# Second block's attention: both compressions in the two halves of the array, and the values' products of two units at once

## The chip, the cores and the metric

The kernel runs on one NeuronCore of a Trainium2 chip. The metric is the device time of one execution in microseconds (us), the median of repeated runs.

## The reference, cut to what matters

Two networks run one after the other on a sequence of 512 tokens of width 1024; the change lies in the second one, `second_block`, which has two layers. Each layer's mixer has four branches of width 512: native sparse attention (`o_a`), a convolution, a pooling mixer, and sliding-window attention (`o_d`).

```python
def nsa_compress(k, pos, w1, w2):              # for the keys and again for the values
    blk = jnp.swapaxes(k[:, idx], 2, 3) + pos  # 31 blocks of 32 positions, 2 groups, 64 channels
    flat = blk.reshape(bsz, n_cmp, g, CMP_LEN * dk)
    return jax.nn.gelu(flat @ w1, approximate=True) @ w2      # 2048 -> 256 -> 64
...
o_cmp, p_cmp = nsa_compressed_attention(qa, k_cmp, v_cmp)
o_slc = nsa_selected_attention(qa_rot, rope(k_slc), v_slc, sel)
o_win = banded_attention(qa_rot, rope(k_win), v_win, NSA_WINDOW, None)
o_a = ga[0] * o_cmp + ga[1] * o_slc + ga[2] * o_win
o_d = banded_attention(qd, rope(k_d), v_d, SWA_WINDOW, sinks)
```

There are 8 query heads of width 64 over 2 groups of keys and values, and all of it is float32.

## The kernel before

Nearly all of the time goes into products with weights. A weight tile of 128x1024 is loaded into one of three `raw` buffers, rounded by ScalarE (line 88, into one of three `whi` buffers), and the rest is formed by VectorE (line 89, into one of three `wlo` buffers). `mm3` (lines 112 to 114) then makes three products for each pair of tiles, hi by hi, hi by lo and lo by hi. A projection (`proj`) is 24 such products of 512 columns for one bank of results; there are four banks (`mm`).

`mix2` is one layer's mixer. It has a first stretch, written out as a list of calls at its end: `compress_inputs` for keys and values, `keys`, `swa_query`, `conv_taps` (a projection pair whose 30 taps VectorE works off in portions, `some(n)`), `pool_part` (a projection, sums on VectorE, then a product at line 1252), `compress`, and `values_and_gates` (the values of all four token tiles and the gates, 96 products of 408 columns in four chunks of weights, lines 1361 to 1372). `compress(kv, ab)` is called for the keys and for the values. It is a generator: up to its first `yield` it loads 16 tiles of `w1` into the `L` and `pT` buffers (four of each) and makes 16 products of a 128x64 stationary tile with 256 columns (line 1405) in rows 0 to 63 of one bank, then the GELU; up to the second it turns the hidden values over (line 1419), up to the third it multiplies with `w2` (lines 1428 and 1433).

Behind it come 48 units of attention: 16 of the sliding window and 32 of the sparse attention. `attend` makes a unit's scores (line 1453) and the softmax; `tail` turns the probabilities over (line 1475) into two `pT` buffers; `times_values` multiplies them with the values (line 1484), group 0 into rows 0 to 63 of the bank `po` and group 1 into rows 64 to 127, in turn. The loop over `n` issues unit n's scores, unit n-1's turning, then a portion of other work (`filling`: one projection or pieces of the gates and branches), then unit n-1's values. `attend_coarse(j)` (lines 1487 to 1516) makes the attention over the compressed keys for four units at once. The build reorders independent instructions on each engine, so the order that counts is that of the built program.

Of the kernel before, what the change touches and what calls it, by code (L numbers as in the profile page):

```python
# [16 lines left out]
P = 128  # L17
# [13 lines left out]
class Net:  # L31
# [1151 lines left out]
    def mix2(self, l, after):  # L1183
# [174 lines left out]
        def values_and_gates():  # L1358

            banks = [self.mm_bank() for _ in n4]  # L1360
            for c in range(4):
                whi, wlo = self.weights(a["w_in_vg_2"][l, :, c * 816:(c + 1) * 816])
                for k, t in [(k, t) for t in n4 for k in range(2)] if c == 3 else [(k, t) for k in range(2) for t in n4]:
                    hi, lo = self.hk(2 * c + k)
                    ws = slice(k * 408, (k + 1) * 408)
                    self.mm3(banks[t][:, :408], (hi[:, sl[t]], lo[:, sl[t]]), (whi[:, ws], wlo[:, ws]),
                             2 * c + k == 0, 2 * c + k == KD - 1)
            for t in n4:
                A.copy(vt[:, t, :], banks[t][:, :384])
                A.activation(ga[t], banks[t][:, 384:408], AF.Tanh, scale=0.5)  # L1370
            V.tensor_scalar(gt_, gt_, 0.5, 0.5, ALU.mult, ALU.add)
            V.tensor_scalar(ga[0][:, :8], ga[0][:, :8], valid, None, ALU.mult)


        kc = mp.tile([P, 64], F32, name=f"kc{l}")
# [17 lines left out]
                                    pos[:, kv, 8 * e:8 * e + 8, None].to_broadcast([P, 8, 32 - e]), ALU.add)  # L1393
            return ab

        def compress(kv, ab):

            ph = self.aux()
            for c in range(8):
                w1 = ltile() if c % 2 else ptile()  # L1400
                nc.sync.dma_start(w1, a["nsa_cmp_w1_2"][l, kv][:, c * 512:(c + 1) * 512])
                for i in range(2):
                    lp = 2 * c + i
                    e = lp // 8
                    T_.matmul(ph[:64, :256], ab[e][:, lp % 8].rearrange("p g n -> p (g n)"), w1[:, i * 256:(i + 1) * 256],  # L1405
                              start=(lp == 0), stop=(lp == 15))
            x = ph[:64, :256]
            t, w2 = gtile(), gtile()
            t = t[:64, :256]
            A.activation(t, x, AF.Square)  # L1410
            V.tensor_scalar(t, t, 0.044715, 1.0, ALU.mult, ALU.add)
            V.tensor_tensor(t, t, x, ALU.mult)
            A.activation(t, t, AF.Tanh, scale=math.sqrt(2.0 / math.pi))
            stt(t, t, 1.0, x, ALU.add, ALU.mult)
            nc.sync.dma_start(w2, a["nsa_cmp_w2_2"][l])
            yield
            pt = self.aux()
            for hf in range(2):
                T_.transpose(pt[:, hf * 64:(hf + 1) * 64], t[:, hf * P:(hf + 1) * P], self.ident[:64, :64])
            both = tmp(2 * P)  # L1420
            A.copy(both.rearrange("p (f r n) -> p f r n", f=2, r=2),
                   pt[:, :P].rearrange("p (f n) -> p f n", f=2)[:, :, None, :].to_broadcast([P, 2, 2, 64]))
            hid = [both[:, sl[hf]] for hf in range(2)]
            yield
            pt = self.aux()
            if kv == 0:
                for hf in range(2):
                    T_.matmul(pt[:, :64], w2[:, sl[hf]], hid[hf][:, :64], start=(hf == 0), stop=(hf == 1))
                for g in range(2):
                    A.mul(kc[halves[g], 32 * g:32 * g + 32], pt[halves[g], 32 * g:32 * g + 32], 0.5)  # L1430
            else:
                for hf in range(2):
                    T_.matmul(pt[:, :64], hid[hf], w2[:, (2 + hf) * P:(2 + hf) * P + 64],
                              start=(hf == 0), stop=(hf == 1))
                for b in range(4):
                    A.mul(vc[32 * b:32 * b + 32, b // 2, 64 * (b % 2):64 * (b % 2) + 64], pt[32 * b:32 * b + 32, :64], 0.5)
            yield

        def ltile():
            return mp.tile([P, 512], F32, tag="L", name=self.nm("L"), bufs=4)  # L1440
# [2 lines left out]
            return mp.tile([P, 512], F32, tag="pT", name=self.nm("pT"), bufs=4)  # L1443

        def attend(qs, ks, k0, w, mask, sinks, gate, vals, po, i, coarse, last):


            mn = mp.tile([P, 4], F32, tag="mn", name=self.nm("mn"), bufs=4)
            cols, Ls = self.packed(), []
            pts = [cols(w) for _ in range(2)]  # L1450
            for g, pt in enumerate(pts):
                for b, k in enumerate(ks):
                    T_.matmul(pt, qs[g][:, sl[i]], k[g][:, k0:k0 + w], start=b == 0, stop=b == 1)  # L1453
            for g, pt in enumerate(pts):
                L, m, s = ltile(), mn[:, 2 * g:2 * g + 1], mn[:, 2 * g + 1:2 * g + 2]
                init = sinks[g] if sinks else 3e38
                V.tensor_tensor_reduce(L[:, :w], pt, mask, scale=1.0, scalar=init, op0=ALU.add, op1=ALU.min, accum_out=m)
                e = w
                if sinks:
                    V.tensor_copy(L[:, w:w + 1], init)  # L1460
                    e += 1
                A.activation(L[:, :e], L[:, :e], AF.Exp, bias=m, scale=-1.0, accum_out=s)
                V.reciprocal(s, s)
                if gate is None:
                    V.tensor_scalar(L[:, :w], L[:, :w], s, None, ALU.mult)
                else:
                    V.tensor_scalar(L[:, :w], L[:, :w], s, gate[g], ALU.mult, ALU.mult)
                Ls.append(L)

            def tail():  # L1470
                pT = []
                for g in range(2):
                    pt = self.aux()
                    for c in range(0, w, P):
                        T_.transpose(pt[:, c:c + P], Ls[g][:, c:c + P], self.ident)  # L1475
                    pT.append(ptile())
                    (V.tensor_copy if g and w > 2 * P else A.copy)(pT[g][:, :w], pt[:, :w])

                def times_values():
                    todo = list(coarse) if coarse else []  # L1480
                    todo += [[(vals(g, b), pT[g][:, b * P:(b + 1) * P]) for g in range(2)] for b in range(w // P)]
                    for b, pair in enumerate(todo):
                        for g, (v, p) in enumerate(pair):
                            T_.matmul(po[halves[g], sl[i]], v, p, start=b == 0 and coarse is not None,  # L1484
                                      stop=last and b == len(todo) - 1)
                return times_values
            return tail
# [89 lines left out]
                taps.pop(0)()  # L1577

        ab = [compress_inputs(kv) for kv in range(2)]
        cmp_ = [compress(kv, ab[kv]) for kv in range(2)]  # L1580
        keys("d", 8)
        swa_query(0)
        conv_taps(0)
        next(cmp_[0])
        pool_part(0)
        some(6)
        swa_query(1)
        next(cmp_[1])
        next(cmp_[0])
        conv_taps(1)  # L1590
        some(6)
        next(cmp_[1])
        next(cmp_[0])
        pool_part(1)
        some(4)
        next(cmp_[1])
        some(4)
        values_and_gates()
        some(4)
        pool_part(2)  # L1600
        pool_part(3)
# [16 lines left out]
        def unit(nsa, j, i, part):  # L1618
            w = (i + 1) * P
            if not nsa:  # L1620
# [1 line left out]
                w -= j0 * P  # L1622
                return attend(queries["d", j], stacks["d"], j0 * P, w, band[:, 2 * P - w:],
                              [sink[:, 4 * g + j:4 * g + j + 1] for g in range(2)], None,
                              lambda g, b: vt[:, j0 + b, 256 + 64 * g:320 + 64 * g], po[-1], i, [], True)
            c = 8 * (part + 1)
            return attend(queries["a", j], stacks["sw"[part]], 0, w, causal[:, S - w:], None,
                          [ga[i][:, c + 4 * g + j:c + 4 * g + j + 1] for g in range(2)],
                          lambda g, b: vt[:, b, part * P + 64 * g:part * P + 64 * g + 64], po[-1], i,
                          None if part else coarse[j][i], part == 1)  # L1630

        units = [(0, j, i, 0) for j in range(4) for i in n4] + \
            [(1, j, i, part) for j in range(4) for i in n4 for part in range(2)]
# [1 line left out]
        fill = [lambda: keys("s", 6)] + fills(2, brc)  # L1635
        at = {4: lambda: swa_query(2), 8: lambda: swa_query(3), 12: lambda: nsa_query(0)}
        at.update({half + 8 * j + 3: lambda j=j: nsa_query(j + 1) for j in range(3)})
        po, o, wait, coarse = [], [], None, {}

        def filling(n, left):  # L1640
            some(2 if n < half else 8)
# [2 lines left out]
            else:  # L1644
                drain(fill, left)

        for n in range(end + 1):
            tail = None
            if n < end:
                nsa, j, i, part = units[n]  # L1650
                if i + part == 0:
                    po.append(self.mm_bank())
                    if nsa:
                        coarse[j] = attend_coarse(j)
                if n == half:
                    keys("w", 7)
                tail = unit(*units[n])
            if wait:
                wait = wait()
            if n < end and n != half:  # L1660
                filling(n, half - n if n < half else end - n)
            if wait:
                wait()
                if n < end and i + part == 0 or n == end:
                    o.append(single(f"o{len(o) % 4}"))
                    A.copy(o[-1], po.pop(0))
            wait = tail
            if n == half:
                brd = [whole(t) for t in o]
# [185 lines left out]
```

## Time and profile before

| | us |
|---|---|
| median of 3 runs | 3513.74 (3510.46 to 3514.96) |
| the profiled execution | 3505.12 |
| its span, first to last instruction | 3503.3 |
| TensorE busy (PE) | 3405.6 (97%) |
| VectorE busy (DVE) | 2110.1 (60%) |
| ScalarE busy (ACT) | 1402.9 (40%) |

A row of the timeline gives the start of a run of equal instructions, how long it lasts, the engine, line, operation, output and inputs, its shape and how many records it has; idle time before it and what ended it stand in brackets. A product of float32 that is not split has two records. Products overlap, so what one costs is the distance from its start to the next start, not its duration.

### The profile page before, as it was taken

The numbers are of one execution on the slowest core, as the hardware profiler recorded it, in microseconds if no ns is written. First come the engines' busy times: TensorE is split into PE (matmuls) and PEld (weight loads), VectorE is DVE, ScalarE is ACT, GpSimd is POOL, SyncE is SP. The second block draws the span as 40 slices with busy tenths as digits, with TensorE's granted clock in tenths as the row PEclk, the third lists the DMA queues.
The fourth block names the chain that finished last, engine by engine and source line by source line (L and its number), as shares of the span: only waits on it lengthen the run. The fifth ranks groups of instructions, "written<-read, shape, count | busy, mean of one in ns | idle before, by whom it ended". The sixth has DMA issues, their size and how long they took to land.

```text
span 3503.3 us, 57134 instructions
## 1 busy us (share of the span) xinstructions
PE 3405.6 (97%) x22898; PEld 2942.7 (84%) x22898; DVE 2110.1 (60%) x3875; ACT 1402.9 (40%) x2907; POOL 182.5 (5%) x316
## 2 busy tenths in 40 slices
PE   6999999999999999999999999999999999999998
PEld 5777889889998888897777788898977777898988
DVE  7667675554456633458966645535589676456364
ACT  3444442233445422333545434434334444354342
POOL 0222100001111000000000000000000000000000
PEclk9999999999999999999999999999999999999999
DMA  6332245643332433343322232222352322232322
GB/s 215 97 98 83 64 150 183 188 137 97 104 91 68 127 93 100 109 154 116 88 88 70 73 136 82 93 96 94 122 161 85 97 73 70 85 120 97 98 97 79
DMA packets 137433, 374.49 MB, mean 107 GB/s; under 512 B 24624, under 2 KB 33664, under 8 KB 137168
## 3 DMA queue, kind: packets, MB, share of 16 engines
q1 hardware_dynamic: 137168, 370.84, 33.7%
q8 instruction: 180, 2.95, 0.3%
q14 instruction: 85, 0.70, 0.1%
HBM read 347.09 MB, written 8.48 MB: 101 GB/s over the span
## 4 chain that ended last, share of the span: by engine, by line
PE 60%; DVE 3%; ACT 1%; issue 1%; POOL 0%; DMA 0%; SPq 0%; DVEq 0%; POOLq 0%; ACTq 0%
PE mm L112 18%; PE mm L114 18%; PE mm L113 18%; PE mm L1484 2%; PE aux L1453 2%; PE aux L1475 1%; DVE cy L1268 1%; DVE wlo L89 1%; ACT aux L133 0%; PE aux L151 0%; DVE x L1142 0%; POOL rs L85 0%; PE aux L1498 0%; PE aux L1252 0%; PE aux L1405 0%
## 5 line engine op out<-in xcount | busy, mean ns | idle before, releaser
L112 PE MATMUL mm<-hhi,whi 128*128 128x512 f32 (+1 forms) x2776 | 1058.6, 382 | 7.9 <-ACT hhi L88 6.4
L114 PE MATMUL mm<-hhi,wlo 128*128 128x512 f32 (+1 forms) x2776 | 1050.5, 379 | 3.1 <-DVE wlo L89 3.1
L113 PE MATMUL mm<-hlo,whi 128*128 128x512 f32 (+1 forms) x2776 | 1051.2, 379 | 0.6 <-DVE hlo L89 0.6
L89 DVE TENSOR_TENSOR wlo<-raw,whi 128x1024 fp32r<-128x1024 f32 (+3 forms) x523 | 594.1, 1136 | 594.9 <-ACT whi L88 587.1
L88 ACT CAST whi<-raw 128x1024 fp32r<-128x1024 f32 (+3 forms) x523 | 512.8, 980 | 1034.4 <-PE mm L113 469.4
L112 PEld LDWEIGHTS mm<-hhi,whi 128*128 128x128 f32 x2776 | 525.4, 190 | 103.1 <-ACT hhi L88 7.2
L114 PEld LDWEIGHTS mm<-hhi,wlo 128*128 128x128 f32 x2776 | 525.7, 189 | 99.9 <-DVE wlo L89 4.2
L113 PEld LDWEIGHTS mm<-hlo,whi 128*128 128x128 f32 x2776 | 525.9, 190 | 94.4 <-DVE hlo L89 2.4
L112 PE MATMUL mm<-whi,hidhi 128*128 128x256 f32 x1056 | 297.2, 281 | 0.0
L114 PE MATMUL mm<-whi,hidlo 128*128 128x256 f32 x1056 | 297.1, 281 | 0.0
L113 PE MATMUL mm<-wlo,hidhi 128*128 128x256 f32 x1056 | 297.1, 281 | 0.0
L112 PE MATMUL mm<-whi,hhi 128*128 128x256 f32 (+1 forms) x736 | 216.0, 294 | 1.5 <-ACT whi L88 1.5
L114 PE MATMUL mm<-whi,hlo 128*128 128x256 f32 (+1 forms) x736 | 213.4, 290 | 0.0
L113 PE MATMUL mm<-wlo,hhi 128*128 128x256 f32 (+1 forms) x736 | 213.0, 289 | 0.0
L113 PEld LDWEIGHTS mm<-wlo,hidhi 128*128 128x128 f32 x1056 | 200.6, 190 | 0.3
L112 PEld LDWEIGHTS mm<-whi,hidhi 128*128 128x128 f32 x1056 | 200.6, 190 | 0.3
L114 PEld LDWEIGHTS mm<-whi,hidlo 128*128 128x128 f32 x1056 | 200.6, 190 | 0.0
L1268 DVE SCALAR_TENSOR_TENSOR cy<-cc,cw,cy 128x497 f32<-128x497 f32 (+19 forms) x240 | 177.4, 749 | 9.1 <-ACT cy L1265 5.3
L112 PEld LDWEIGHTS mm<-whi,hhi 128*128 128x128 f32 x736 | 140.7, 191 | 3.1 <-ACT whi L88 1.9
L113 PEld LDWEIGHTS mm<-wlo,hhi 128*128 128x128 f32 x736 | 140.9, 191 | 0.4 <-DVE wlo L89 0.2
L114 PEld LDWEIGHTS mm<-whi,hlo 128*128 128x128 f32 x736 | 140.7, 191 | 0.5 <-DVE hlo L89 0.2
L1164 DVE SCALAR_TENSOR_TENSOR fy<-mm,fcw,fy 128x511 f32<-128x511 f32 (+1 forms) x176 | 131.2, 746 | 3.0
(386 smaller groups left out, 5075.2 us busy)
## 6 DMA issues: line engine op xcount, KB each, us to landing
raw<-in_w_ffn_in_dram SPq DMA_DIRECT2D x88, 512.0 KB, 3.8
raw<-in_ffn_w_up_dram SPq DMA_DIRECT2D x88, 512.0 KB, 3.2
raw<-in_w_ada_dram SPq DMA_DIRECT2D x80, 512.0 KB, 3.8
raw<-in_w_gate_dram SPq DMA_DIRECT2D x64, 512.0 KB, 3.2
raw<-in_w_in_dram SPq DMA_DIRECT2D x50, 512.0 KB, 3.7
raw<-in_gdn_w_in_dram SPq DMA_DIRECT2D x32, 512.0 KB, 3.8
raw<-in_w_ffn_out_dram SPq DMA_DIRECT2D x32, 512.0 KB, 3.6
raw<-in_w_branch_dram SPq DMA_DIRECT2D x64, 256.0 KB, 2.6
```

The costliest lines, as they stand in the source:

```text
L88: self.nc.scalar.copy(hi, src)
L89: self.nc.vector.tensor_tensor(lo, src, hi.bitcast(F32), ALU.subtract)
L112: mm(out, ahi, bhi, start=first, stop=False)
L113: mm(out, ahi, blo, start=False, stop=False)
L114: mm(out, alo, bhi, start=False, stop=last)
L1164: stt(y[:, d:], bank[:, :S - d], cw[:, j, 2 - d:3 - d], y[:, d:], ALU.mult, ALU.add)
L1268: taps.append(lambda d=d: stt(y[:, d:], c[:, :S - d], cw[:, f, 30 - d:31 - d], y[:, d:], ALU.mult, ALU.add))
L1453: T_.matmul(pt, qs[g][:, sl[i]], k[g][:, k0:k0 + w], start=b == 0, stop=b == 1)
L1475: T_.transpose(pt[:, c:c + P], Ls[g][:, c:c + P], self.ident)
L1484: T_.matmul(po[halves[g], sl[i]], v, p, start=b == 0 and coarse is not None, stop=last and b == len(todo) - 1)
```

## The change

`compress(ab)` now does keys and values together: the keys' products go to rows 0 to 63 of the bank and the values' to rows 64 to 127, in turn, and everything behind them is done once on 128 rows. It yields after every two chunks, and `values_and_gates` yields after each of its four chunks of weights; both are called in turn, right behind `pool_part(0)`. In the loop over the units the values' products of two units are issued together, at every even n, and `attend_coarse` comes behind them. Line numbers move: 1405 becomes 1410, 1419 becomes 1426, 1453 becomes 1459, 1475 becomes 1481, 1484 becomes 1490.

```diff
         def values_and_gates():
...
+                if c < 3:
+                    yield
...
+            yield
-        def compress(kv, ab):
+        def compress(ab):
             ph = self.aux()
             for c in range(8):
-                w1 = ltile() if c % 2 else ptile()
-                nc.sync.dma_start(w1, a["nsa_cmp_w1_2"][l, kv][:, c * 512:(c + 1) * 512])
+                ws = [ltile(), ptile()]
+                for kv in range(2):
+                    nc.sync.dma_start(ws[kv], a["nsa_cmp_w1_2"][l, kv][:, c * 512:(c + 1) * 512])
                 for i in range(2):
                     lp = 2 * c + i
                     e = lp // 8
-                    T_.matmul(ph[:64, :256], ab[e][:, lp % 8].rearrange("p g n -> p (g n)"), w1[:, i * 256:(i + 1) * 256],
-                              start=(lp == 0), stop=(lp == 15))
+                    for kv in range(2):
+                        T_.matmul(ph[halves[kv], :256], ab[kv][e][:, lp % 8].rearrange("p g n -> p (g n)"),
+                                  ws[kv][:, i * 256:(i + 1) * 256], start=(lp == 0), stop=(lp == 15))
+                if c % 2 and c < 7:
+                    yield
...
                 def times_values():
-                    todo = list(coarse) if coarse else []
+                    todo = coarse() if coarse else []
...
-        cmp_ = [compress(kv, ab[kv]) for kv in range(2)]
+        cmp_ = compress(ab)
         keys("d", 8)
         swa_query(0)
         conv_taps(0)
-        next(cmp_[0])
         pool_part(0)
         some(6)
+        values = values_and_gates()
+        for _ in range(4):
+            next(values)
+            next(cmp_)
         swa_query(1)
-        next(cmp_[1])
-        next(cmp_[0])
+        some(4)
         conv_taps(1)
         some(6)
-        next(cmp_[1])
-        next(cmp_[0])
+        next(cmp_)
         pool_part(1)
         some(4)
-        next(cmp_[1])
-        some(4)
-        values_and_gates()
+        next(cmp_)
         some(4)
         pool_part(2)
         pool_part(3)
...
                 tail = unit(*units[n])
             if wait:
-                wait = wait()
+                turned.append(wait())
             if n < end and n != half:
                 filling(n, half - n if n < half else end - n)
-            if wait:
-                wait()
-                if n < end and i + part == 0 or n == end:
+            if n and n % 2 == 0:
+                while turned:
+                    turned.pop(0)()
+                if n == end or i + part == 0:
                     o.append(single(f"o{len(o) % 4}"))
                     A.copy(o[-1], po.pop(0))
+            if n < end and nsa and i + part == 0:
+                coarse[j] = attend_coarse(j)
             wait = tail
```

On TensorE, the first block of compression products in the first layer (`q` are the inputs, `pT` and `L` tiles of `w1`). Before, every product of the block goes to the same 64 rows, two for each tile of `w1`:

```order
L1405 MATMUL aux_16000<-pT_16001,q_15862 64x256 x2
L1405 MATMUL aux_16000<-L_16005,q_15862 64x256 x2
L1405 MATMUL aux_16000<-pT_16009,q_15862 64x256 x2
L1405 MATMUL aux_16000<-L_16013,q_15862 64x256 x2
L1405 MATMUL aux_16000<-pT_16017,q_15863 64x256 x2
```

Now, in the second of the layer's four groups, keys (`L`) and values (`pT`) take turns, and the third chunk of the values' projection follows:

```order
L1410 MATMUL aux_16089<-L_16136,q_15862 64x256
L1410 MATMUL aux_16089<-pT_16137,q_15877 64x256
L1410 MATMUL aux_16089<-L_16144,q_15862 64x256
L1410 MATMUL aux_16089<-pT_16145,q_15877 64x256
L1410 MATMUL aux_16089<-L_16144,q_15862 64x256
L1410 MATMUL aux_16089<-pT_16145,q_15877 64x256
L112 MATMUL mm_16055<-whi_16153,hhi_15440 128x408
L113 MATMUL mm_16055<-wlo_16154,hhi_15440 128x408
```

The four blocks of 16 products in the program have become eight groups of eight.

On TensorE among the units of the sliding window. Before, each unit's products with the values (`v`) stand alone, ahead of the next scores (`kst` by `q`):

```order
L1484 MATMUL mm_16721<-pT_16989,v_15848 64x128
L1484 MATMUL mm_16721<-pT_16994,v_15848 64x128
L1484 MATMUL mm_16721<-pT_16989,v_15848 64x128
L1484 MATMUL mm_16721<-pT_16994,v_15848 64x128
L1453 MATMUL aux_17057<-kst_15900,q_16139 128x256
```

Now those of two units (four `pT` tiles) stand together:

```order
L1490 MATMUL mm_16708<-pT_16902,v_15848 64x128
L1490 MATMUL mm_16708<-pT_16907,v_15848 64x128
L1490 MATMUL mm_16708<-pT_16902,v_15848 64x128
L1490 MATMUL mm_16708<-pT_16907,v_15848 64x128
L1490 MATMUL mm_16708<-pT_16972,v_15848 64x128
L1490 MATMUL mm_16708<-pT_16977,v_15848 64x128
L1490 MATMUL mm_16708<-pT_16972,v_15848 64x128
L1490 MATMUL mm_16708<-pT_16977,v_15848 64x128
L1459 MATMUL aux_17044<-kst_15900,q_16305 128x256
```

Counted over the whole order, line 1484's 108 separate groups are 56 at line 1490, with the same 496 products; 76 groups of scores stood right behind one, and 34 do now.

On VectorE behind the GELU of the compression (line 1421), where now the splits of three weights (`wlo`, for `pool_part` 1 to 3) stand ahead of `swa_query(1)`'s and `conv_taps(1)`'s work:

```order
L1421 SCALAR_TENSOR_TENSOR gate_16254<-gate_16254,aux_16089 128x256
L89 TENSOR_TENSOR wlo_16400<-raw_16398,whi_16399 128x1024
L1302 TENSOR_TENSOR tmp_16297<-tmp_16293,cos_15816 128x512
L89 TENSOR_TENSOR wlo_16469<-raw_16467,whi_16468 128x1024
L1304 TENSOR_TENSOR tmp_16295<-tmp_16297,tmp_16296 128x512
L1320 TENSOR_TENSOR q_16307<-tmp_16295,q_16305 64x512
L1320 TENSOR_TENSOR q_16307<-tmp_16295,q_16306 64x512
L89 TENSOR_TENSOR wlo_16520<-raw_16518,whi_16519 128x1024
L1264 SCALAR_TENSOR_TENSOR cc_16380<-cc_16380,mm_16324 128x512
```

Before, the values' 96 products lay between `pool_part(1)` and `pool_part(2)`; now `swa_query(1)`, `conv_taps(1)` and three pool parts follow each other.

## Rows read from the trace of the kernel before

**Rows 1.** the page, part 1: busy us, share of the span, instructions.

```profile
PE 3405.6 (97%) x22898; PEld 2942.7 (84%) x22898; DVE 2110.1 (60%) x3875; ACT 1402.9 (40%) x2907; POOL 182.5 (5%) x316
```

**Rows 2.** busy time: two stretches of layer one, 8 us of layer two.

```profile
core 0: us, PE busy (x) PEld busy (x) DVE busy (x) ACT busy (x) POOL busy (x), PEclk, DMA share, GB/s
1562.00:1664.00 102.00, 98.92 (x449) 78.55 (x448) 89.20 (x131) 34.15 (x57) 4.23 (x14) 1.00 0.40 132
1664.00:2084.00 420.00, 416.52 (x2319) 331.33 (x2318) 285.54 (x701) 190.26 (x441) 14.08 (x16) 1.00 0.27 83
2556.00:2564.00 8.00, 4.73 (x14) 3.42 (x14) 6.67 (x11) 2.89 (x4) 0.00 (x0) 0.79 0.88 255
```

**Rows 3.** timeline, PE: the first compression block of the first layer.

```profile
1561.68 0.39 PE L113 MATMUL mm<-hlo,whi 128*128 128x512 f32 x1
1561.90 0.39 PE L114 MATMUL mm<-hhi,wlo 128*128 128x512 f32 x1
1562.22 1.08 PE L1405 MATMUL aux<-pT,q 128*64 128x256 f32 x4
...
1568.32 1.03 PE L1405 MATMUL aux<-L,q 128*64 128x256 f32 x4
1569.27 0.50 PE L112 MATMUL mm<-hhi,whi 128*128 128x512 f32 x1
```

**Rows 4.** line 1405: duration ns min/median/max, first and last start.

```profile
L1405 PEld LDWEIGHTS aux<-pT,q x64: 133/137/137, 1562.2 to 2578.9; 128*64 128x64 f32 x64
```

**Rows 5.** timeline, PE: one unit's values in 8 records, scores behind.

```profile
1677.45 0.39 PE L114 MATMUL mm<-hhi,wlo 128*128 128x512 f32 x1
1677.77 0.66 PE L1484 MATMUL mm<-pT,v 128*64 128x128 f32 x8
1678.36 0.74 PE L1453 MATMUL aux<-kst,q 128*128 128x256 f32 x4
1678.94 0.41 PE L1475 MATMUL aux<-ident,L 128*128 128x128 f32 x2
```

**Rows 6.** timeline, PE: one unit's values in 20 records.

```profile
1953.87 0.44 PE L1484 MATMUL mm<-pTc,vc 128*64 128x128 f32 x4
1954.14 1.04 PE L1484 MATMUL mm<-pT,v 128*64 128x128 f32 x16
1955.12 0.55 PE L1498 MATMUL aux<-kc,q 128*128 128x64 f32 x3
```

**Rows 7.** timeline, PE: scores behind a projection.

```profile
1669.66 0.64 PE L1453 MATMUL aux<-kst,q 128*128 128x256 f32 x4
1670.14 0.38 PE L1475 MATMUL aux<-ident,L 128*128 128x128 f32 x2
```

**Rows 8.** timeline, PE: the second layer's first block and what follows.

```profile
2547.35 1.08 PE L1405 MATMUL aux<-pT,q 128*64 128x256 f32 x4
...
2554.19 1.08 PE L1405 MATMUL aux<-pT,q 128*64 128x256 f32 x4 [0.71 <-DMA pT<-in_nsa_cmp_w_dram]
...
2557.67 0.50 PE L112 MATMUL mm<-hhi,whi 128*128 128x512 f32 x1 [1.54 <-ACT whi L88]
...
2560.14 0.79 PE L114 MATMUL mm<-hhi,wlo 128*128 128x512 f32 x1 [1.73 <-DVE wlo L89]
2560.73 0.63 PE L112 MATMUL mm<-hhi,whi 128*128 128x512 f32 x1
```

**Rows 9.** waits of PE, 1562 to 1664: us in total, times, longest.

```profile
PE aux L1252 <- DVE tmp L1250: 1.7, 2, 1.5
PE mm L114 <- DVE wlo L89: 1.3, 1, 1.3
```

**Rows 10.** VectorE by line, 1562 to 1664: busy us, mean ns, idle before.

```profile
L1268 DVE SCALAR_TENSOR_TENSOR cy<-cc,cw,cy 128x511 f32<-128x511 f32 (+14 forms) x69 | 52.1, 756 | 4.2 <-ACT cy L1265 2.7
L89 DVE TENSOR_TENSOR wlo<-raw,whi 128x1024 fp32r<-128x1024 f32 (+1 forms) x17 | 19.8, 1168 | 5.9 <-ACT whi L88 5.9
L1244 DVE TENSOR_TENSOR tmp<-tmp 128x512 f32<-128x512 f32 x10 | 6.9, 687 | 0.1
```

More of the change, by code (lines that the diff above doesn't have):

```diff
@@ L1404, in compress @@
                     e = lp // 8
-                    T_.matmul(ph[:64, :256], ab[e][:, lp % 8].rearrange("p g n -> p (g n)"), w1[:, i * 256:(i + 1) * 256],
-                              start=(lp == 0), stop=(lp == 15))
-            x = ph[:64, :256]
+                    for kv in range(2):
[3 more added lines that the diff above has]
+                    yield
+            x = ph[:, :256]
             t, w2 = gtile(), gtile()
-            t = t[:64, :256]
+            t = t[:, :256]
             A.activation(t, x, AF.Square)
@@ L1418, in compress @@
             for hf in range(2):
[L1419 to L1423, printed above, removed]
+                T_.transpose(pt[:, sl[hf]], t[:, sl[hf]], self.ident)
+            hk, hv = tmp(P), tmp(2 * P)
+            pf = pt[:, :2 * P].rearrange("p (f n) -> p f n", f=2)
+            A.copy(hk.rearrange("p (f n) -> p f n", f=2), pf[:, :, :64])
+            A.copy(hv.rearrange("p (f r n) -> p f r n", f=2, r=2), pf[:, :, None, 64:].to_broadcast([P, 2, 2, 64]))
             yield
             pt = self.aux()
[L1426 to L1436, printed above, removed]
+            for hf in range(2):
+                T_.matmul(pt[:, :64], w2[:, sl[hf]], hk[:, 64 * hf:64 * hf + 64], start=(hf == 0), stop=(hf == 1))
+            for hf in range(2):
+                T_.matmul(pt[:, 64:P], hv[:, sl[hf]], w2[:, (2 + hf) * P:(2 + hf) * P + 64], start=(hf == 0), stop=(hf == 1))
+            for g in range(2):
+                A.mul(kc[halves[g], 32 * g:32 * g + 32], pt[halves[g], 32 * g:32 * g + 32], 0.5)
+            for b in range(4):
+                A.mul(vc[32 * b:32 * b + 32, b // 2, 64 * (b % 2):64 * (b % 2) + 64], pt[32 * b:32 * b + 32, 64:P], 0.5)
             yield
@@ L1624, in unit @@
                               [sink[:, 4 * g + j:4 * g + j + 1] for g in range(2)], None,
-                              lambda g, b: vt[:, j0 + b, 256 + 64 * g:320 + 64 * g], po[-1], i, [], True)
+                              lambda g, b: vt[:, j0 + b, 256 + 64 * g:320 + 64 * g], po[-1], i, 0, True)
             c = 8 * (part + 1)
@@ L1629, in unit @@
                           lambda g, b: vt[:, b, part * P + 64 * g:part * P + 64 * g + 64], po[-1], i,
-                          None if part else coarse[j][i], part == 1)
+                          None if part else lambda: list(coarse[j][i]), part == 1)
         units = [(0, j, i, 0) for j in range(4) for i in n4] + \
@@ L1637, in mix2 @@
         at.update({half + 8 * j + 3: lambda j=j: nsa_query(j + 1) for j in range(3)})
-        po, o, wait, coarse = [], [], None, {}
+        po, o, wait, coarse, turned = [], [], None, {}, []
         def filling(n, left):
@@ L1652, in mix2 @@
                     po.append(self.mm_bank())
-                    if nsa:
-                        coarse[j] = attend_coarse(j)
                 if n == half:
```

## Prediction, made before the changed kernel ran

> **What bounds it.** I read the page's busy times first, then the busy time by stretch, then TensorE's timeline at the places that the change touches, and its waits. TensorE is busy in 97% of the span [rows 1], and so it is in both stretches of the mixer: 98.9 of 102 us in the first, 416.5 of 420 among the units, at a granted clock of 1.00 [rows 2]. So a microsecond less of products is a microsecond less of time, unless another engine falls behind. The one to fear is VectorE: it is busy 89.2 of the first stretch's 102 us [rows 2]. What a group of products costs is the distance between starts. A projection's products follow each other in 0.23 us (1561.68 to 1561.90) [rows 3].
>
> **Compression products.** A block of line 1405 runs from 1562.22 to 1569.27 us, 7.05 us for 32 records, 0.22 each, and the product before it is followed after 0.32 us instead of 0.23, an entry of 0.09 [rows 3]. The program has four blocks, two in each layer: 4 x 7.14 = 28.6 us without waits. All of it goes into one half of the array's columns, the stationary tile being 64 wide. Line 1484 already alternates between two such halves: 20 records take 1.25 us (1953.87 to 1955.12) [rows 6] and 8 take 0.59 (1677.77 to 1678.36) [rows 5], so a further record costs (1.25 - 0.59) / 12 = 0.055 us, a pair 0.11. A record there has 128 columns, half of line 1405's 256, and alone should cost half of 0.22, that is 0.11. The pair costs what one costs: the halves run at the same time. So I take 0.22 us for a pair at line 1410.
>
> A group also has a fixed cost. Eight records at 0.055 are 0.44, the group takes 0.59, and the entry is 0.09 again (1677.45 to 1677.77) [rows 5]: 0.15 + 0.09 = 0.24 us. Each new group has 8 products, 16 records, 8 pairs: 8 x 0.216 + 0.24 = 1.97 us (0.216 is 7.05 less the group's ends, over 32). Eight groups: 15.8 us. **Gain 12.8 us.** The other end, no overlap at all, is a rival below. The extra four groups are in this sum.
>
> The page "TensorE: Matmul & The Clock Gate" of the Trainium skill says in its Part 3 (packing small matmuls) that a weight load overlaps running products only if it goes to another group of rows; here all tiles use all 128 rows. By that, the load of 0.137 us [rows 4] would stand beside each pair and the eight groups would take 8 x (8 x 0.353 + 0.24) = 24.5 us, a gain of 4.1. But line 1484's pair, over the same 128 rows, takes 0.11 us [rows 5, 6], less than one load, so there the loads are hidden. I go by the rows.
>
> **Values' products.** The order lists 108 groups before and 56 after, with the same products. 52 groups fewer at 0.24: **gain 12.5 us.** Scores right behind a values' group also start late: they take 0.58 us (1678.36 to 1678.94) [rows 5] and 0.48 behind a projection (1669.66 to 1670.14) [rows 7]. Of 76 such groups 34 stay; of the 42 some are pieces of a split group, so I take 32 x 0.10: **gain 3.2 us** (bounds 0 and 4.2).
>
> **What I cost at nothing.** The small turnings and products behind the GELU, the `w1` loads (as many bytes, 16 tiles a layer, each needed later than before), half of the GELU's vector work, two wider copies: all are off TensorE or below 1 us. The pairing needs four `pT` tiles and has four: unit n's turning writes those that the pair before it has read. `attend_coarse` moves behind the pair; its results are first read two units later, so its chain on VectorE keeps a projection of cover.
>
> **Old waits that go.** In the first layer the projection behind the first block waits 1.3 us for its split weights [rows 9]. In the second the block itself lasts from 2547.35 to 2557.67, 10.3 us instead of 7.05, with waits for `w1` tiles and then for the rounded weights, and 1.7 us more follow for the split ones; behind them the products have 0.63 us instead of 0.39, the granted clock of that stretch being 0.79, on the way between its levels of 1.2 and 2.4 GHz [rows 2, 8]. That is 3.3 + 1.7 + some 1.5 for the low clock. All of it comes from weights of `pool_part(0)` that were queued on SP behind `w1` tiles; in the new order that load stands ahead of them, and the compression comes a projection and a chunk of values later. **Gain 8 us** (bounds 0 and 8).
>
> **New waits.** The values no longer lie between the pool parts. From the end of `swa_query(1)`'s products to the last pool product TensorE has five projections (5 x 24 x 0.23 = 27.6), 35 further products (8.0) and small ones (some 3): 38.5 us. VectorE's order has in the same stretch 6 splits at 1.17, 15 taps at 0.76, 9 window sums at 0.69 [rows 10] and 16 others, about 8 us: 32.5. And the second and third split of the last listing of the order wait for a `whi` buffer, that is for the projection three before and a cast behind it, while the rope and the taps queue up behind them; I estimate 6 us idle. 32.5 + 6 = 38.5 against 38.5, so VectorE just arrives in time, and each of the three pool products and the first unit's turning may wait about a microsecond. The nearest rows are the pool products' waits of today, two with 1.7 in total [rows 9]. I take 3.5 us a layer, 7 in all, less the waits of the same kind that they replace: 1.7 in the first layer [rows 9] and, as an estimate, 0.8 in the second. **Loss 4.5 us**; bounds 0 and 5.5 us (a whole projection) at each of the eight places less what goes, 41.
>
> **Sum.** -12.8 - 12.5 - 3.2 - 8 + 4.5 = -32 us. On the profiled execution's own 3505.1 that gives 3473. That execution lies 8.6 us below the median of the runs shown, 3513.7; on the median the forecast is **3482 us**.
>
> **Rivals.** (1) *The halves do not overlap at line 1410.* For it: nothing in the trace has 256 columns in both halves. Against: line 1484 does it with 128 [rows 5, 6]. Eight groups of 16 x 0.216 + 0.24 = 3.7 us are 29.6, a loss of 1 instead of a gain of 12.8: sum -18, 3496. By the page's rule, gain 4.1, the sum would be -23 and the time 3490. Chance 0.04 and 0.03.
> (2) *VectorE becomes the bound of the first stretch.* For it: 89.2 of 102 us are busy [rows 2], and the split weights stand ahead in its queue. If that stretch kept its old length, the compression's gain and the old waits would be given back and only the values' 12.5 + 3.2 stay: 3498. Against: the taps are filler and can slide among the units. Chance 0.10.
> (3) *Slower: the held splits stop TensorE itself.* Place: the three splits behind the GELU. If each wait there passed through whole, a projection of 5.5 us at four places in two layers is 44 us, the gains without the 4.5 are 36.5, and the time would be 3514 + 7.5 = 3521. It decides once the new waits exceed 18 us a layer. Against: 1.5 us is the longest such wait now [rows 9], with VectorE as busy as it will be. Chance 0.02.
>
> **How the numbers follow.** Forecast 0.81, the rivals 0.04, 0.03, 0.10 and 0.02. The forecast's own bounds: without the old waits' gain 3490, with no new waits 3477; both sizes of overheads could be off by a quarter (7 us). I take 3469 to 3502, which reaches over rivals 1 and 2. A measurement of this kernel can tell about 0.2%, 7 us, from no change. Faster by more than that: 0.94 (all but rival 3 and a larger form of rival 2); the same 0.04; slower 0.02.
>
> **What would show it.** Line 1410 in eight groups of about 1.9 us, starts in pairs 0.22 apart; a lone 0.22 per record means rival 1, about 0.35 per pair the page's rule. 56 groups of line 1490, each longer by 0.055 per record. No wait for `w1` and no clock below 1.00 in the second layer's first stretch. Waits at line 1252 or at the first turning of the units, up to a microsecond each; if they are 3 or more, or line 114 waits for `wlo`, rival 2 or 3 is at work. The prediction is wrong if the first stretch keeps its 102 us, or if the values' groups come apart on the chip.

## The result, and the profile after

The changed kernel takes **3475.65 us** (median of 4 runs, 3466.12 to 3479.28), the kernel before 3512.1 us beside it (4 runs, 3507.95 to 3514.96): a ratio of **0.9894, 95% interval 0.9873 to 0.9915**. In two later comparisons on other occasions it was 0.9888 (0.9866 to 0.9909) and 0.989 (0.9873 to 0.9908). The forecast was 3482, range 3469 to 3502.

The page's first part of the changed kernel, which answers to [rows 1]:

```profile
PE 3383.6 (97%) x22894; PEld 2946.0 (85%) x22894; DVE 2103.2 (60%) x3869; ACT 1403.9 (40%) x2903; POOL 183.2 (5%) x316
```

TensorE is still busy in 97% of the span, now a shorter one. To see where the time went, the span is cut at the same landmarks in both kernels. Busy times by stretch of the kernel before: in order, the last turning of the first layer's norm up to its first scores, from there to its last values' product, the same two of the second layer, and the first 500 us of the program; behind the length of a stretch, each engine's busy time and count, then the granted clock of TensorE (1.00 is full speed), the DMA share and GB/s.

```profile
1533.60:1663.70 130.10, 127.03 (x639) 104.59 (x638) 103.00 (x155) 42.62 (x71) 5.54 (x15) 1.00 0.49 153
1663.70:2016.40 352.70, 351.42 (x2038) 278.61 (x2037) 259.38 (x669) 170.95 (x413) 14.08 (x16) 1.00 0.27 80
2520.90:2652.10 131.20, 126.46 (x620) 103.17 (x619) 103.57 (x156) 43.02 (x71) 6.16 (x15) 0.99 0.48 147
2652.10:3004.80 352.70, 351.33 (x2038) 278.56 (x2036) 258.19 (x669) 172.34 (x414) 14.23 (x16) 1.00 0.27 80
...
0.00:500.00 500.00, 445.70 (x4737) 373.91 (x4738) 350.42 (x719) 228.12 (x630) 78.68 (x158) 0.97 0.36 115
```

The same view of the changed kernel, and 8 us of the second layer that answer to the last row of [rows 2]:

```profile
1542.60:1663.70 121.10, 119.89 (x638) 100.25 (x637) 96.57 (x145) 42.38 (x70) 5.92 (x15) 1.00 0.54 162
1663.70:2007.10 343.40, 341.73 (x2033) 279.00 (x2031) 261.38 (x676) 171.68 (x413) 15.19 (x16) 1.00 0.27 81
2515.50:2634.10 118.60, 117.82 (x618) 97.99 (x617) 96.24 (x146) 42.19 (x69) 5.10 (x15) 1.00 0.52 161
2634.10:2978.00 343.90, 342.04 (x2032) 279.02 (x2031) 262.36 (x676) 173.20 (x414) 14.02 (x16) 1.00 0.28 81
...
0.00:500.00 500.00, 444.99 (x4696) 372.94 (x4697) 344.76 (x712) 225.15 (x626) 79.01 (x158) 0.94 0.35 111
2556.00:2564.00 8.00, 8.00 (x49) 6.92 (x49) 6.76 (x10) 1.75 (x2) 0.00 (x0) 1.00 0.97 354
```

The first stretches give 130.1 - 121.1 = 9.0 and 131.2 - 118.6 = 12.6 us, the units 9.3 and 8.8. TensorE has 5 and 6 instructions fewer there (2038 against 2033 and 2032): some projection products moved behind the last values, so the stretch behind it is 1.1 us longer in each layer (113.07 to 114.12, 111.55 to 112.67), and the units' real gain is 8.2 and 7.7. Together 37.5 us, close to what the timed runs show (36.5). The two profiled spans differ by only 25.8 us (3503.3 and 3477.5): this execution of the changed kernel lost some 9 us ahead of the first mixer, in the same code, at a granted clock of 0.94 in the first 500 us where the other had 0.97, and 3 us between the layers.

The timeline of TensorE in the changed kernel, the first joint compression group (start, us, engine and line; in square brackets what it waited for). It answers to [rows 3]:

```profile
1583.30 1.13 PE L1252 MATMUL aux<-tmp,pw 128*128 128x512 f32 x2 [1.20 <-DVE tmp L1250]
1584.35 0.43 PE L1410 MATMUL aux<-L,q 128*64 128x256 f32 x1
1584.36 0.43 PE L1410 MATMUL aux<-pT,q 128*64 128x256 f32 x1
1584.62 0.38 PE L1410 MATMUL aux<-L,q 128*64 128x256 f32 x1
1584.63 0.38 PE L1410 MATMUL aux<-pT,q 128*64 128x256 f32 x1
...
1585.92 0.38 PE L1410 MATMUL aux<-L,q 128*64 128x256 f32 x1
1585.92 0.38 PE L1410 MATMUL aux<-pT,q 128*64 128x256 f32 x1
1586.23 0.45 PE L114 MATMUL mm<-whi,hlo 128*128 128x408 f32 x1
...
1677.08 0.88 PE L1490 MATMUL mm<-pT,v 128*64 128x128 f32 x12
1677.88 0.74 PE L1459 MATMUL aux<-kst,q 128*128 128x256 f32 x4
```

The keys' record (`L`) and the values' record (`pT`) start 0.01 us apart, and the pairs follow each other in 0.22. From 1584.35 to 1586.23 the group takes 1.88 us, and so do the other seven. A weight load of this line lasts 0.137 us:

```profile
L1410 PEld LDWEIGHTS aux<-L,q x64: 132/137/137, 1584.4 to 2574.9; 128*64 128x64 f32 x64
```

The last two lines of the timeline are two units' values in one group: 12 records in 0.80 us, where 8 took 0.59 before [rows 5].

The waits of TensorE in the two first stretches of the changed kernel (total, times, longest), which answer to [rows 8, 9]. One row per layer is all that there is:

```profile
PE aux L1252 <- DVE tmp L1250: 1.2, 1, 1.2
...
PE aux L1252 <- DVE tmp L1250: 0.8, 1, 0.8
```

In the kernel before, the second layer's first stretch had these:

```profile
PE mm L114 <- DVE wlo L89: 1.7, 1, 1.7
PE mm L112 <- ACT whi L88: 1.5, 1, 1.5
PE aux L1405 <- DMA pT<-in_nsa_cmp_w_dram: 0.7, 1, 0.7
PE aux L1405 <- POOL tmp L1239: 0.6, 1, 0.6
PE aux L1252 <- DVE tmp L1250: 0.2, 1, 0.2
```

No wait is left for `w1` tiles, rounded or split weights, and the 8 us that had a clock of 0.79 [rows 2] now have 1.00.

### The profile page after: what moved, and what is told of

Read it like the earlier page. It is cut to its first block, busy times and chain, and to the rows that moved or that the text cites. A ratio compares the mean times of both kernels' runs of the same rounds, so it can differ in the third digit from the quotient of the medians.

```text
span 3477.5 us, 57130 instructions
## 1 busy us (share of the span) xinstructions
PE 3383.6 (97%) x22894; PEld 2946.0 (85%) x22894; DVE 2103.2 (60%) x3869; ACT 1403.9 (40%) x2903; POOL 183.2 (5%) x316
## 4 chain that ended last, share of the span: by engine, by line
PE 89%; DVE 5%; ACT 3%; issue 2%; POOL 1%; DMA 0%; SPq 0%; DVEq 0%; POOLq 0%; ACTq 0%
PE mm L112 26%; PE mm L113 25%; PE mm L114 25%; PE mm L1490 2%; PE aux L1459 1%; PE aux L1481 1%; DVE cy L1268 1%; PE aux L151 1%; PE aux L687 1%; PE aux L977 1%; DVE wlo L89 1%; PE aux L614 1%; ACT aux L133 0%; PE mm L1010 0%; PE aux L1000 0%
## 5 line engine op out<-in xcount | busy, mean ns | idle before, releaser
L89 DVE TENSOR_TENSOR wlo<-raw,whi 128x1024 fp32r<-128x1024 f32 (+2 forms) x523 | 594.9, 1138 | 574.1 <-ACT whi L88 564.9
L88 ACT CAST whi<-raw 128x1024 fp32r<-128x1024 f32 (+2 forms) x523 | 512.9, 981 | 1027.9 <-PE mm L113 447.7
L1268 DVE SCALAR_TENSOR_TENSOR cy<-cc,cw,cy 128x487 f32<-128x487 f32 (+23 forms) x240 | 175.0, 749 | 5.8 <-ACT cy L1265 3.5
L1468 ACT ACTIVATE L<-L,mn 128x129 f32<-128x129 f32 (+5 forms) x192 | 102.1, 534 | 81.6 <-DVE mn L1463 76.2
```

Of the source, the lines that this page charges most:

```text
L88: self.nc.scalar.copy(hi, src)
L89: self.nc.vector.tensor_tensor(lo, src, hi.bitcast(F32), ALU.subtract)
L1268: taps.append(lambda d=d: stt(y[:, d:], c[:, :S - d], cw[:, f, 30 - d:31 - d], y[:, d:], ALU.mult, ALU.add))
```

## The experiments

Theory: the pairs of halves run at the same time and each group of products in halves costs 0.24 us beside its products; the pieces of the values' projection cover weights and pools. Rivals: the gain comes from something that merely moved, or the order of issue in the halves does not matter.

**The changed kernel again**, twice, beside the experiments.

> The changed kernel itself, once more, with more rounds. Its first profile is 25.8 us shorter than that of before, its runs 36.5 us, while the mixers' stretches alone are 39.7 us shorter; there the clock fell more often in the first 450 us, where the code is the same. If that is chance, as I think, the ratio stays at 0.989 to 0.990 (35 to 39 us), and the time before the first layer's compression is within 3 us of that of before in this profile or the clock shows the difference. Rival: the new kernel has a lasting loss elsewhere; then the same 10 us or so of low clock come back in the first 450 us.

Ratio 0.9888 (0.9866 to 0.9909); stretches 121.07, 343.36, 118.76 and 343.71 us.

> The changed kernel once more, beside the two others on the same chip. Theory: ratio to the kernel before 0.989, the stretches 121.1 and 118.8 us, the units 343.5 us a layer.

Ratio 0.989 (0.9873 to 0.9908); stretches 121.10, 343.37, 118.34 and 343.95 us. The stretches and ratios are as expected. The loss ahead of the first mixer does not stay: the norm's last turning, which was at 1533.6 us in the kernel before and at 1542.6 in the changed kernel's first profile, is at 1537.8 and 1532.3 us in these two, with a clock of 0.96 and 0.97 in the first 500 us. In the first of them the 4.2 us are more than the 3 that were expected, at a lower clock than the 0.97 of the kernel before.

**The two parts apart.** The values of two units together, with the compression and the values' projection as before:

```
+                turned.append(wait())
...
+            if n and n % 2 == 0:
+                while turned:
+                    turned.pop(0)()
...
```

> The kernel before with nothing but the values of two units issued together (and the coarse attention behind them). The theory that each group of values' products costs 0.24 us to enter and leave, and 0.1 us for scores right behind it: 52 groups fewer, 15.6 us less in the stretch of the units, the first stretch as before (130 us each), a time 15 to 16 us below that of before (ratio 0.9955). Rival: the units are held by the softmax on the vector and scalar engines, and what the products give up comes back as waits: under 5 us.

Ratio 0.995 (0.9931 to 0.9969), 3490.35 us. The units' stretches are 343.55 and 343.39 us, the whole of the change's; the first stretches are 132.39 and 132.45 us, as before the change or slightly longer.

The joint compression and the split projection, with each unit's values by themselves:

```
...
-            if n and n % 2 == 0:
-                while turned:
-                    turned.pop(0)()
...
+            if wait:
+                wait()
...
```

> The changed kernel with the values' products issued for each unit again, as before. The parts add up: 21.7 us less, all of it in the first stretches (about 121 and 119 us from the last turning of the norm to the first scores instead of 130 and 131), the units' stretch as before, a ratio of 0.994. Rival: the parts do not add, since the first stretch is bound by the vector engine and only pays because the units behind it are shorter: under 15 us.

Ratio 0.9935 (0.9914 to 0.9956), 3485.32 us; first stretches 121.10 and 119.09 us, units 351.98 and 352.23. The parts add: 0.0050 + 0.0065 = 0.0115 against the 0.0112 of both beside them.

**Is it the turn of the halves?** Within each group, four of the keys' products and then four of the values', so eight records and eight:

```
-                for i in range(2):
...
-                    for kv in range(2):
...
+                for kv in range(2):
+                    for m in range(4):
...
```

> The changed kernel with the same products in each compression group, but the four of the keys first and then the four of the values, instead of in turn. If the two halves run at the same time only where their products alternate in the queue, a group takes nearly 16 x 0.216 + 0.24 = 3.5 to 3.7 us instead of 1.88, 13 us more in all: ratio to before 0.993. Rival: the gain of the compression comes from its new place between the values' chunks, or the queue looks far enough ahead to overlap blocks; then the group stays near 2 us and the time at the changed kernel's.

Ratio 0.9901 (0.9883 to 0.992), first stretches 124.75 and 122.27 us: 3.65 us more a layer. By time alone this kernel cannot be told from the change (0.9888 beside it). Both expectations missed the group's length. TensorE's timeline of this kernel, one group:

```profile
1580.22 1.29 PE L1412 MATMUL aux<-L,q 128*64 128x256 f32 x5
1581.14 0.43 PE L1412 MATMUL aux<-pT,q 128*64 128x256 f32 x1
1581.35 0.38 PE L1412 MATMUL aux<-L,q 128*64 128x256 f32 x1
...
1581.84 1.24 PE L1412 MATMUL aux<-pT,q 128*64 128x256 f32 x5
1583.01 0.45 PE L112 MATMUL mm<-whi,hhi 128*128 128x408 f32 x1
```

Four records of the keys run alone, the fifth starts with the values' first (1581.14), four pairs run together, and four of the values run alone at the end. The group takes 2.79 us, between 1.88 (all pairs) and 3.5 (none). A reading of it: products in the two halves overlap only as far as the engine sees the other half's record in its queue. Here the values' first record is the fourth behind the keys' fifth. The next kernel tests that: two products and two by turns, so blocks of four records.

```
-                for i in range(2):
...
-                    for kv in range(2):
...
+                for kv in range(2):
+                    for i in range(2):
...
```

> The changed kernel with two products of the keys and then two of the values by turns, where the change takes one by one and the kernel of the blocks took four by four. Theory (TensorE looks a few records ahead in its queue: in blocks of eight records the values' first record started beside the keys' fifth, the fourth record ahead of it): with blocks of four records the values' first starts beside the keys' first, a group takes 1.88 us as in the change, and the first stretches are 121.1 and 118.6 us. Rival (the second half of a block overlaps, whatever its length): two records alone, two pairs, two alone, so 2.3 to 2.8 us a group and first stretches 2 to 4 us longer.

TensorE's timeline of this kernel, the first group:

```profile
1582.76 0.43 PE L1409 MATMUL aux<-L,q 128*64 128x256 f32 x1
1582.77 0.43 PE L1409 MATMUL aux<-pT,q 128*64 128x256 f32 x1
1583.03 0.38 PE L1409 MATMUL aux<-L,q 128*64 128x256 f32 x1
1583.04 0.38 PE L1409 MATMUL aux<-pT,q 128*64 128x256 f32 x1
...
1584.69 0.45 PE L114 MATMUL mm<-whi,hlo 128*128 128x408 f32 x1
```

The values' first record starts with the keys' first, and the group takes 1.93 us, with first stretches of 121.23 and 118.64 us: a look ahead of four records fits all three orders, "the second half of a block overlaps" does not. The runs show when records start, not the queue itself, so the look-ahead is a reading that fits and not a thing that was seen. One time, 3474.07 us.

**Where the values' projection stands.** Back in one piece at its old place, with the joint compression in four groups of 16 products:

```
-        values = values_and_gates()
-        for _ in range(4):
-            next(values)
+        for _ in range(2):
             next(cmp_)
...
+        for _ in values_and_gates():
+            pass
```

> The changed kernel with the projections of values and gates in one piece at their old place behind the second part of the pools; keys and values are still compressed together in the two halves, now in four groups of 16 products, and the units are those of the change. Theory (the split pieces cover the weights' transfers and the pools): the weights of the second pair of groups come late again and the pools are waited for as before, so that the stretch from the norm's last turning to the first scores is some 3 to 4 us longer in each layer than the 121.1 and 118.8 us of the change: about 124.5 and 122.5 us, ratio to the kernel before about 0.991, with a wait for the weights' tiles at the compression's products that the profile names. Rival (the place does not matter, the products alone bring the gain): the two stretches stay within 1 us of 121.1 and 118.8 us and the ratio is that of the change, 0.989.

Ratio 0.9926 (0.9911 to 0.9941), 3484.41 us against 3472.03 of the change beside it. The first stretches are 126.47 and 125.65 us, 5.4 and 7.1 to 7.3 longer, more than the 3 to 4 expected: the rival falls. The waits of TensorE in this kernel's two first stretches:

```profile
PE mm L112 <- ACT whi L88: 3.4, 1, 3.4
PE aux L1252 <- DVE tmp L1250: 1.8, 2, 1.0
...
PE aux L1252 <- DVE tmp L1250: 6.3, 3, 5.6
```

Busy time of the second of them:

```profile
2514.20:2639.80 125.60, 119.32 (x618) 98.88 (x617) 103.70 (x153) 42.40 (x69) 5.50 (x15) 0.97 0.50 152
```

No `w1` tile is waited for, so that detail of the expectation is wrong: TensorE waits for a rounded weight and for the pools' vector work instead, and in the second layer's stretch the clock falls to 0.97 in the mean. The projection's pieces in their new place are worth some 12 us here, as cover for other engines' work. The place and the cut into four pieces changed together, so the run does not tell one from the other.

**What the remaining wait is for.** The first part of the pools ahead of the convolution's first part:

```
+        pool_part(0)
         conv_taps(0)
-        pool_part(0)
```

> The changed kernel with the first part of the pools ahead of the convolution's first part instead of behind it, and nothing else. Theory (the wait of 1.2 and 0.8 us ahead of the pools' first product is for VectorE's chain, which starts 24 products earlier here): the wait goes, and the first stretches are 119.5 to 120.1 us in layer 1 and 117.5 to 118 us in layer 2 instead of 121.1 and 118.6. Rival (VectorE has too much queued ahead of the compression, so that the wait only moves to the convolution's or the keys' steps): both stretches stay within 0.5 us, or are longer, with a wait elsewhere. By time alone the two do not differ from the change's 0.989 by more than a run can tell.

Busy times of the two first stretches of this kernel:

```profile
1536.60:1656.50 119.90, 119.89 (x638) 100.20 (x637) 94.53 (x145) 42.05 (x70) 5.02 (x15) 1.00 0.53 163
2508.30:2625.80 117.50, 117.48 (x619) 98.03 (x618) 95.83 (x146) 42.11 (x69) 5.06 (x15) 1.00 0.53 162
```

The wait is gone: TensorE is busy 119.89 of 119.90 us and 117.48 of 117.50. The cause of the wait was the order of VectorE's work. By time, 0.9897 (0.9875 to 0.992), the 2.3 us are not to be seen.

**Fewer groups still.** The values of four units behind one another, where narrow units' turned weights share a buffer; 32 groups instead of 56:

```
+                both = ptile() if w <= 2 * P else None
...
-            if n and n % 2 == 0:
+            if n and n % 4 == 0 or n > half and n % 8 == 6:
```

> The changed kernel with the values' products of four units behind one another where their turned weights find room (units of up to 256 columns put both groups' weights into one buffer): 32 groups of values' products instead of 56 in both layers. Theory (each group of products in the two halves costs some 0.24 us beside its products, and the scores right behind it 0.10 us): 24 x 0.24 + 16 x 0.10 = 7.4 us less, the units' stretch about 340 us a layer instead of 343.5, ratio to the kernel before about 0.987. Rival (with the values later, their softmax steps or the banks of the sums are waited for, or TensorE runs out of turned weights): the units' stretch stays at 343.5 us or grows, with waits at the scores or at the values that the profile names.

> The changed kernel with the values of four units behind one another where they fit, a second time beside the others. The units' stretch is 341.0 to 341.4 us a layer as in its first profile, 4.9 us less than the change's in both layers, so the ratio to the kernel before should be 0.987 to 0.988.

Ratios 0.9879 (0.986 to 0.9898) and 0.9904 (0.9884 to 0.9923), on either side of the change's own 0.989. Waits of TensorE in the first layer's units of this kernel:

```profile
PE aux L1520 <- DVE Lc L1517: 1.1, 1, 1.1
PE aux L1482 <- DVE L L1471: 0.7, 1, 0.7
PE aux L1482 <- ACT gate L1548: 0.7, 1, 0.7
PE aux L1459 <- DVE mn L1463: 0.4, 1, 0.4
PE aux L1482 <- ACT whi L88: 0.4, 1, 0.4
PE aux L1290 <- ACT pT L1484: 0.3, 1, 0.3
```

The units' stretches are 341.01 and 341.35 us, 2.4 and 2.5 less than the change's rather than 3.7. From each group's first start to the next start behind it, the first layer's groups took 32.74 us together in the change and take 29.82 here. These 2.9 us look like 12 x 0.24, but the 0.09 of an entry lie ahead of the first start: 12 groups at 0.15 are 1.8. Most of the rest comes from pieces of the change that are gone here, four with a single product and so no partner, and one group of 16 records that took 1.78 us where such a group usually takes 1.02. The fixed cost itself held for longer groups:

```profile
1686.77 1.75 PE L1491 MATMUL mm<-pT,v 128*64 128x128 f32 x28
1688.45 0.74 PE L1459 MATMUL aux<-kst,q 128*128 128x256 f32 x4
```

28 records take 1.68 us, and 0.15 + 28 x 0.055 are 1.69. But the waits above, 3.6 us in all where the change has 1.3 in that stretch, took part of the gain back: for the most part softmax steps are late, at the scores and the turnings (lines 1459, 1482 and 1520).

> The two together: the first part of the pools ahead of the convolution's, and the values of four units behind one another where they fit. If both hold, the first stretches are some 2 us shorter than the change's in all and the units' stretches 4.9 us, so a ratio of 0.987 to the kernel before; if only the units hold, 0.988.

3470.77 us, ratio 0.9894 (0.9872 to 0.9916). By its stretches (119.88, 340.95, 117.52 and 341.39 us) it is 7.2 us shorter than the change, the best of all. By time it cannot be told from the change, whose runs on one occasion spread over 15 us (3464.36 to 3479.63).

## Why the prediction came out as it did

**Compression products: right.** Eight groups of 1.88 us and an entry of 0.09 were forecast at 1.97 each, and that is what they take. Rival 1 falls: the pairs are 0.22 us apart with two loads of 0.137 us each, so neither "no overlap" nor the rule of the Trainium skill ("TensorE: Matmul & The Clock Gate", Part 3, a load overlaps only with other row groups) describes these halves of columns. Where records of one half run alone, in the blocks of four products, they stand 0.23 us apart in the mean, so a pair does cost what one costs. What I had not seen is that the overlap hangs on the turn: by blocks of four products it would have cost 7.3 us of the gain.

**Values' products and scores: right.** Forecast -15.7 us, measured 8.2 + 7.7 = 15.9, and the kernel with this part alone shows the same stretches. The fixed cost of a group, read from two group sizes, also held for groups of 28 records.

**Old waits that go: right.** None of the waits of [rows 8, 9] for weights is left, and the low clock went with them. Together with the new waits, TensorE's idle time in the two first stretches fell from 7.8 to 2.0 us. With the projection at its old place the waits come to 11.5 us, so it is its new place that takes them away, apart from those for `w1` tiles, which are gone there too.

**New waits: mis-sized, and by another mechanism.** The term was 7 us less 2.5 that go, a loss of 4.5. Measured are 1.2 + 0.8 = 2.0 us, against the pool waits of 1.7 and 0.2 in the old order: no loss at all. The step that failed is "VectorE just arrives in time, and each of the three pool products and the first unit's turning may wait". None of these four waits. The one that does is the first pool product, ahead of the compression, and it goes when VectorE gets that work earlier. The 6 us of idle VectorE in that estimate came from no row. The term makes most of the difference between 32 forecast and 37.5 found in the stretches; the rest is smaller, among it four turnings of 128 columns behind the GELU where there were eight of 64, some 0.4 us a layer that I had costed at nothing.

**Rival 2** falls with it: VectorE is busy 96.57 of the first layer's 121.1 us, and TensorE waits 1.2. **Rival 3** is far off in this order, but a wait of its size exists: with the projection at its old place a single pool product waits 5.6 us, for the pools' vector work and not for a split.

The median of 3475.65 lies 6 us below the forecast, about the size of the one wrong term; a measurement of this kernel can hardly tell so little apart.

## What to carry to other kernels

Small products that fill half of the array's columns cost next to nothing beside a partner in the other half, if the two are issued by turns or in short blocks (here up to four records), and each group of them has a fixed price, so gather them into few, long groups. Read that price from two sizes of group in the trace (here 0.24 us) before writing a line. A block of ordinary products moved between small dependent steps is worth as much as what it covers: here four pieces of it in a new place were worth some 12 us, about a third of the whole gain.

## What had not been expected of the hardware

In these runs products in the two column halves ran together only when the other half's record was close behind in the queue: with blocks of four records all pairs overlapped (1.93 us a group), with blocks of eight only half (2.79), and in that block the overlap began exactly four records ahead. Records of the two halves also did not start in the order of the built program: there the values' first record started at 1581.14 us and the keys' sixth, three places ahead of it, at 1581.35. Longer blocks were not tried, nor other widths. And the same code ahead of the mixer took 9 us longer in one profiled execution than in another, at a granted clock of 0.94 instead of 0.97 over 500 us, so that spans of single profiles mislead where stretches do not. Why the clock differed stays open.
